# All projections first, one attention pipeline for both sequences, local attention together with the output projection

## The chip, the cores and the metric

The kernel runs on one core of one Trainium2 chip. The metric is the device time of one execution in microseconds (us). The core has a matrix engine, TensorE (PE in the profile; PEld is its loading of weights), and three engines for elementwise work: VectorE (DVE), ScalarE (ACT) and GpSimd (POOL). SyncE (SP) issues the transfers between device memory and the on-chip memory; all of this kernel's transfers stand in its queue. Each engine works off its own instructions in order and waits on semaphores for the others.

## The reference

One encoder layer is applied to two sequences, a prompt of 1024 tokens (s = 0) and a sample of 2048 tokens (s = 1), each with its own condition vector `c`; all data are float32, the model width is 1024. For each sequence:

```python
mod = silu(c) @ w_ada + b_ada
shift, scale, gate = split(mod, 3)
proj = (x * (1 + scale) + shift) @ w_in            # 1024 -> 3328 columns
qa, ka, va, ga, qb, kb, vb, gb = split(proj, ...)  # 512, 128, 128, 512, 4 x 512
oa = window_gqa(qa, ka, va, sink, rel_bias) * silu(ga)
ob = diff_attention(qb, kb, vb, lambdas, subln_w, rel_bias) * silu(gb)
h = concat(oa, ob) @ w_out
y = layer_norm(ALPHA * x + gate * h, ln_g, ln_b)
```

The local attention `window_gqa` has 8 query heads and 2 key heads of 64; a block of 128 queries sees the blocks before, at and after it (384 keys), with a bias by distance, a mask beyond 128 and a sink logit per head that only enters the denominator. The differential attention has 4 heads; each makes two softmaxes over the whole sequence, takes `p0 - lam * p1`, multiplies it with 128 value columns, and normalises the result by its root mean square.

## The kernel before

**Precision.** Each float32 operand of a matmul is split into a high part and a rest (names ending in H and L), and a product is three matmuls: high x high, high x low, low x high. So beside every matmul there is an elementwise split, a copy on ACT and a subtraction on DVE or POOL.

**Stages.** (1) The condition vector becomes shift and scale; tokens are transposed, modulated and split (`build_u`). (2) `projections` runs over three column passes (the prompt, then the two halves of the sample), each over 13 groups of 256 output columns and two blocks of 512 tokens. It is a Python generator whose steps are three matmuls (`step3`, L185 to L187); results go to device memory (`store`). The first pass is run as one piece. (3) `diff_attention(0, ...)` handles the prompt, with three projection steps (`filler(3)`) ahead of each attention step. (4) `window_attention` handles local attention in blocks of 128 queries, in two halves of four heads each: `first` makes logits (L767), adds bias and takes the maximum (L770), takes Exp (L773), and scales by the reciprocal (L791); `second`, one half later, transposes (L810), splits, multiplies with the values (L804, L805), adds the parts of the product (L823, L826), multiplies with the gate (L829) and writes to device memory (OT). Projection steps stand between its parts (`fill(2)`). (5) `diff_attention(1, ...)` handles the sample; it begins among the last projections, and from then on has no filler. One of its blocks (128 queries of one head, L636 to L688) takes four steps on TensorE: logits, values of an earlier pair of blocks, transposes of the block three before. (6) The output projection reads OT, forms the differential half (L929, L930), splits the row block (L936 on ACT, L937 on POOL), multiplies with w_out (L947 to L949), adds the residual and normalises.

**What sets the order.** On TensorE the order is that of the code (`manual_schedule`), so what stands between two attention steps there is written by hand. On the other engines a scheduler orders the instructions at build time. Buffers come from pools of a fixed number of tiles, so a load waits until the last reader of the tile before it is done. The prompt's attention has pools of its own, and local attention and the output projection each open theirs after the pools before them are closed.

Of the kernel before, what the change touches and what calls it, by code (L numbers as in the profile page):

```python
# [66 lines left out]
def hybrid_layer(ctx, tc, x_prompt, x_sample, c_prompt, c_sample, w_in, w_out, w_ada, b_ada, ln_g, ln_b,  # L67
# [28 lines left out]
    for s, S in enumerate(SEQS):  # L96
# [7 lines left out]
        GB.append([dt_([P, S], f"gb{s}_{i}") for i in range(4)])  # L104
        OT.append(dt_([KC, P, S], f"ot{s}"))
# [144 lines left out]
    def store(a, s, t0, kind, i):  # L250
# [8 lines left out]
        elif kind == "vA":  # L259
            vf = ev_p.tile([P, CH], F32, tag="eH", name="vf")  # L260
            nc.vector.tensor_copy(vf, a)
# [289 lines left out]
    def diff_attention(s, lag, filler, early, between, bl, bk, bv, bq, b0, b1, bp, be, bw):  # L551

        S = SEQS[s]
        T = S // P
        NQ = S // CH
        NH = S // 1024
        NJ = 2 * NH
        QG = 256
        NG = HB * T // 2
        LC = min((T - 2) * P, 1024)  # L560
        WL = 2 * LC + 384
        sd = "right" if between else None
        ps_lg = Ring("ps_lg", *bl)
        k_p, q_p, w_p, r1_p, r0_p = Ring("kq", *bk), Ring("q", *bq), Ring("W", *bw), Ring("r1", *b1), Ring("r0", *b0)
        with ExitStack() as st:
            st_p = pool(ctx if between else st, "stat", 8, side=sd)
            for r in (k_p, q_p, w_p, r1_p, r0_p):
                r.open(st, sd)
# [3 lines left out]
            def load_head(h):  # L572
                W = w_p.tile([P, WL], F32, name="W")
                nc.sync.dma_start(out=W[:, LC:LC + 384], in_=toeplitz(HA + h, 1)[:, 0])
                for c0, src in ((0, LC), (LC + 384, LC + 383)):
                    if sum(bw) == 1:
                        nc.scalar.copy(W[:, c0:c0 + LC], W[:, src:src + 1].to_broadcast([P, LC]))
                    else:
                        nc.gpsimd.tensor_scalar(out=W[:, c0:c0 + LC], in0=W[:, src:src + 1].to_broadcast([P, LC]),
                                                scalar1=1.0, scalar2=1.0, op0=ALU.mult, op1=ALU.mult)  # L580
                Kt = []
                for kq in range(NQ):
# [4 lines left out]
                heads[h] = (W, Kt, [])  # L587

            def load_values(h):
                Vt = heads[h][2]  # L590
                for kq in range(NQ):
# [8 lines left out]

            def load_group(gg):
                h, g = divmod(gg, T // 2)
                gs = slice(g * QG, (g + 1) * QG)
# [5 lines left out]
                groups_[gg] = {"Q": Q, "s0": s0g, "PT": []}  # L609

            def logits(t, j):

                gg, b = divmod(t, 2)
                h, g = divmod(gg, T // 2)
                if j == 0 and b == 0:
                    if g == 0:
                        load_head(h)
                    load_group(gg)
                    if t == 0:
                        filler(25 if between else 4)  # L620
                G = groups_[gg]
                W, Kt, _ = heads[h]
                if j == 0:
                    units[t] = {"nm": st_p.tile([P, 2, 2], F32, tag="nm", name="nm"),
                                "s1": st_p.tile([P, 4], F32, tag="s1", name="s1")}
                U = units[t]
                m, hf = 1 - j // NH, j % NH
                if hf == 0:
                    U[m] = (r1_p if m else r0_p).tile([P, S], F32, name=f"l{m}")
                i = g * 2 + b  # L630
# [7 lines left out]
                off = (T - 1 - i) * P + hf * 1024 - (T - 2) * P + LC  # L638
# [21 lines left out]
            def transpose(t, kq):  # L660
                gg, b = divmod(t, 2)
                qs = slice(b * P, (b + 1) * P)
                if b == kq == 0 and gg % (T // 2) == 0:
                    load_values(gg // (T // 2))
                if b == 0:
                    groups_[gg]["PT"].append((pt_p.tile([P, 4, QG], F32R, tag="pth", name="pth"),
# [60 lines left out]
            with tc.manual_schedule(engines={PE}):  # L727
                for n in range(early):
                    slot(n, 5)
                if between:  # L730
                    between()
# [284 lines left out]
```

## Time and profile before

| | |
|---|---|
| median of 3 runs | 2158.64 us (2157.99 to 2159.78) |
| the profiled execution | 2160.91 us; its span, from first to last instruction, 2159.1 us |
| TensorE busy | 2072.7 us (96%), 11597 matmuls |
| DVE, ACT, POOL busy | 1435.0, 1055.3, 1122.8 us (66, 49, 52%) |
| mean granted TensorE clock | 0.989 of 2.4 GHz |
| stages, as TensorE shows them | first pass to 341 us; prompt's attention with projections to 691; local attention with projections to 1243; last projections and first blocks of the sample to 1340; sample's attention to about 1850; output projection to 2159 |

A matmul's record is longer than the time after which the next can start, so that records overlap and the busy time is their union. In the lists a row begins with the line of the kernel; `a<-b,c` names the tile that is written and those that are read. Releasers behind an arrow are what ended an engine's idle time.

### The profile page before, as it was taken

What the parts mean: (1) busy time and instruction counts of PE and PEld (TensorE: products, weight loads), DVE (VectorE), ACT (ScalarE), POOL (GpSimd) and SP (SyncE); (2) the same over time, 40 slices, a digit from 0 to 9 for tenths busy, and PEclk for the clock granted to TensorE, in tenths of its full rate; (3) what the DMA queues carried; (4) which work ended last, traced back from release to release, by engine and by line L of the source; (5) the groups of instructions that cost most, each with busy time, mean ns of one, the idle gap of its engine ahead of it and who ended that gap; (6) DMA issues with size and microseconds to landing.
All of it is one profiled execution on the core that took longest, in us unless ns stands there. A gap on an engine that the chain in (4) does not pass through costs nothing. (4 is left out here: it accounts for less than half of the span.)

```text
span 2159.1 us, 32652 instructions
## 1 busy us (share of the span) xinstructions
PE 2072.7 (96%) x11597; PEld 1778.1 (82%) x11597; DVE 1435.0 (66%) x2753; ACT 1055.3 (49%) x1998; POOL 1122.8 (52%) x780
## 2 busy tenths in 40 slices
PE   7999999998999899999999999999999999899997
PEld 4777898787787798888888987999999999777776
DVE  6334126564562586576566845999999999578887
ACT  6211115454452475455555734777777777422221
POOL 3214125554553232332232334889898888756665
PEclk9999999999999999999999999999999999999999
DMA  9675645554557876585768634123151221756663
GB/s 277 182 279 149 176 132 174 122 115 108 126 116 146 182 210 180 168 202 154 182 165 215 167 112 121 43 85 76 40 115 50 60 67 33 201 175 196 194 177 115
DMA packets 315242, 312.45 MB, mean 145 GB/s; under 512 B 31702, under 2 KB 271990, under 8 KB 314696
## 3 DMA queue, kind: packets, MB, share of 16 engines
q1 hardware_dynamic: 315080, 310.37, 53.2%
q8 instruction: 92, 1.51, 0.4%
q14 instruction: 70, 0.57, 0.1%
HBM read 212.70 MB, written 97.60 MB: 144 GB/s over the span
## 5 line engine op out<-in xcount | busy, mean ns | idle before, releaser
L185 PE MATMUL pj<-uH,wH 128*128 128x512 f32 x1040 | 421.0, 405 | 8.0 <-DVE gg L256 4.8
L187 PE MATMUL pj<-uH,wL 128*128 128x512 f32 x1040 | 410.3, 395 | 0.0
L186 PE MATMUL pj<-uL,wH 128*128 128x512 f32 x1040 | 409.5, 394 | 0.0
L636 PE MATMUL lg<-kt,Q 128*128 128x512 f32 x1280 | 372.5, 412 | 19.5 <-DMA kt<-kb 13.0
L658 POOL TENSOR_TENSOR l<-l,l 128x1024 f32<-128x1024 f32 (+1 forms) x192 | 390.1, 2053 | 0.0
L647 ACT ACTIVATE l<-l,nm 128x2048 f32<-128x2048 f32 (+1 forms) x192 | 330.9, 1723 | 31.3 <-DVE nm L640 31.3
L216 POOL TENSOR_TENSOR wL<-wr,wH 128x1024 fp32r<-128x1024 f32 x74 | 181.7, 2457 | 280.0 <-DVE wH L214 201.3
L656 POOL TENSOR_SCALAR l<-l,s 128x1024 f32<-128x1024 f32 (+1 forms) x192 | 186.3, 983 | 193.5 <-DVE s L651 135.6
L640 DVE CUSTOM_DVE_ANT_0 l<-lg,W 128x1024 f32<-128x1024 f32 x192 | 233.7, 1217 | 64.9 <-PE lg L636 32.9
L674 ACT CAST pth<-tp 128x512 fp32r<-128x512 f32 x320 | 186.1, 582 | 177.8 <-PE tp L672 174.8
L636 PEld LDWEIGHTS lg<-kt,Q 128*128 128x128 f32 x1280 | 222.1, 190 | 58.0 <-DMA kt<-kb 8.7
L185 PEld LDWEIGHTS pj<-uH,wH 128*128 128x128 f32 x1040 | 197.7, 190 | 44.3 <-DVE gg L256 5.7
L187 PEld LDWEIGHTS pj<-uH,wL 128*128 128x128 f32 x1040 | 197.1, 190 | 44.2
L675 DVE TENSOR_TENSOR ptl<-tp,pth 128x512 fp32r<-128x512 f32 x320 | 209.0, 685 | 30.9 <-ACT pth L674 30.9
L186 PEld LDWEIGHTS pj<-uL,wH 128*128 128x128 f32 x1040 | 198.0, 190 | 34.1
L672 PE MATMUL tp<-ident,l 128*128 128x128 f32 x1280 | 193.3, 274 | 3.3 <-DVE ptl L675 3.3
L791 POOL TENSOR_SCALAR l<-l,rcA 128x384 f32<-128x384 f32 (+1 forms) x96 | 59.9, 635 | 243.3 <-DVE rcA L784 173.5
L688 PE MATMUL ac<-pth,vt 128*128 128x256 f32 x640 | 182.2, 285 | 0.2 <-DMA vt<-vb 0.2
L687 PE MATMUL ac<-ptl,vt 128*128 128x256 f32 x640 | 181.6, 284 | 0.6 <-DVE ptl L675 0.6
L686 PE MATMUL ac<-pth,vt 128*128 128x256 f32 x640 | 181.3, 283 | 0.5 <-DMA vt<-vb 0.5
L640 DVE CUSTOM_DVE_ANT_0 l<-lg,W,nm 128x1024 f32<-128x1024 f32 x128 | 164.0, 1282 | 24.9 <-PE lg L636 17.8
L770 DVE CUSTOM_DVE_ANT_0 l<-lgA,tA,nsink 128x384 f32<-128x384 f32 (+1 forms) x192 | 113.7, 593 | 81.6 <-PE lgA L767 77.4
(157 smaller groups left out, 4169.8 us busy)
## 6 DMA issues: line engine op xcount, KB each, us to landing
wr<-in_w_in SPq DMA_DIRECT2D x39, 1024.0 KB, 6.8
KAt<-ka SPq DMA_DIRECT2D x40, 384.0 KB, 6.4
Q<-qb SPq DMA_DIRECT2D x96, 128.0 KB, 3.3
Q<-qb SPq DMA_DIRECT2D x48, 256.0 KB, 3.1
kt<-kb SPq DMA_DIRECT2D x24, 512.0 KB, 4.6
vt<-vb SPq DMA_DIRECT2D x48, 256.0 KB, 5.7
QAt<-qa SPq DMA_DIRECT2D x24, 512.0 KB, 7.4
oraw<-ot SPq DMA_DIRECT2D x12, 1024.0 KB, 6.0
```

Source lines behind the costliest of these rows:

```text
L185: nc.tensor.matmul(acc, lhsT=a(k), rhs=b(k), start=(k == 0), stop=False)
L186: nc.tensor.matmul(acc, lhsT=a(k), rhs=bl(k), start=False, stop=False)
L187: nc.tensor.matmul(acc, lhsT=al(k), rhs=b(k), start=False, stop=(k == KC - 1))
L636: nc.tensor.matmul(L[:, c * CH:(c + 1) * CH], lhsT=G["Q"][:, v, m, qs], rhs=Kt[hf * 2 + c][:, m, :], start=(v == 0), stop=(v == 1))
L640: nc.vector.tensor_tensor_reduce(out=row[:, hf * 1024:(hf + 1) * 1024], in0=L, in1=W[:, off:off + 1024], scale=1.0, scalar=3e38 if hf == 0 ...
L647: nc.scalar.activation(row, row, AF.Exp, bias=nm[:, m, NH - 1:NH], scale=-1.0, accum_out=sums)
L656: nc.gpsimd.tensor_scalar(out=U[1][:, cs], in0=U[1][:, cs], scalar1=s1[:, 2:3], scalar2=1.0, op0=ALU.mult, op1=ALU.mult)
L658: nc.gpsimd.tensor_tensor(out=row[:, cs], in0=row[:, cs], in1=U[1][:, cs], op=ALU.add)
L672: nc.tensor.transpose(pt[:, c * P:(c + 1) * P], units[t][0][:, kb * P:(kb + 1) * P], ident)
L674: nc.scalar.copy(H[:, :, qs], p3)
L675: nc.vector.tensor_tensor(out=L[:, :, qs], in0=p3, in1=H[:, :, qs].bitcast(F32), op=ALU.subtract)
L688: nc.tensor.matmul(a, lhsT=Vt[kq][:, 1, c, :], rhs=H[:, c, :], start=False, stop=(kb == T - 1))
```

## The change

The order of the stages becomes: the first pass, then all of the second and nine groups of the third pass alone; then one differential attention pipeline over the blocks of both sequences, sample first, whose first blocks are mixed with the last four projection groups as before; then local attention and output projection in one loop over 24 blocks of 128 tokens. In that loop block t makes its logits and softmax, block t - 1 its transposes and values, and block t - 2 its output projection. OT's window half no longer goes through device memory: the gate product is split into `oH` and `oL` on the spot. The output projection works on 128 tokens at a time, so its loads are halved and doubled in number. Smaller edits go with it: the factor 0.5 of the window's gate moves into va, the norm's weight `wsub` into rows of w_out, the sink becomes the first element of the row that Exp sums, and the scalings of the softmax go to POOL and ACT alone.

```diff
-    diff_attention(0, 2, fill, 0, None, (1, 0), (2, 0), 2, (2, 0), (3, 0), (2, 0), 3, 1, (1, 0))
...
-            window_attention(wp, tA, 0, range(8))
-            project_until(1, 13)
-            window_attention(wp, tA, 1, range(7))
-            project_until(2, 5)
-            window_attention(wp, tA, 1, range(7, 16))
...
-    diff_attention(1, 3, fill, 3, projected, (1, 1), (4, 2), 5, (2, 0), (3, 1), (3, 0), 7, 2, (1, 1))
+    with tc.manual_schedule(engines={PE}):
+        project_until(1, 13)
+        project_until(2, 9)
+    xst.close()
+    diff_attention((1, 0), 3, 3, projected)
...
+        blocks = [(s, h, i) for s in order for h in range(HB) for i in range(SEQS[s] // P)]
...
             def slot(n, extra):
+                gg, ph = divmod(n - lag - 2, 2)
+                nl, nt = steps_of(n), steps_of(n - lag)
+                nv = steps_of(2 * gg) if 0 <= gg < N // 2 else 0
+                for j in range(max(nl, nt, nv, 2)):
+                    if extra:
+                        fill(extra)
+                    if j < nl:
                         logits(n, j)
+                    if j < nv:
+                        values(gg, ph * nv + j)
+                    if j < nt:
                         transpose(n - lag, j)
...
+        def load_weights(k):
+            for n in range(2):
+                ns = slice(n * 512, (n + 1) * 512)
+                raw = wr_p.tile([P, 512], F32, tag="wr", name="raw")
+                nc.sync.dma_start(out=raw, in_=w_out[k * P:(k + 1) * P, ns])
+                if k >= 4:
+                    nc.vector.tensor_scalar(out=raw, in0=raw, scalar1=wsub, scalar2=None, op0=ALU.mult)
+                nc.scalar.copy(woH[k][:, ns], raw)
+                nc.gpsimd.tensor_tensor(out=woL[k][:, ns], in0=raw, in1=woH[k][:, ns].bitcast(F32), op=ALU.subtract)
...
+                if h4 == 3:
+                    rc = sA_p.tile([P, 4], F32, tag="rc", name="rcA")
+                    nc.vector.reciprocal(out=rc, in_=sm_)
+                    for q in range(4):
+                        lv, r1 = l[:, q, 1:1 + nk], rc[:, q:q + 1]
+                        if q == 1:
+                            nc.scalar.activation(lv, lv, AF.Copy, scale=r1)
+                        else:
+                            nc.gpsimd.tensor_scalar(out=lv, in0=lv, scalar1=r1, scalar2=1.0, op0=ALU.mult, op1=ALU.mult)
+                yield
...
             if n == 1:
                 nc.gpsimd.tensor_tensor(out=og, in0=og, in1=B["G"], op=ALU.mult)
+                split(B, 0, og)
...
+        def split(B, half, o):
+            if "oH" not in B:
+                B["oH"] = o_p.tile([P, KC, P], F32R, tag="oH", name="oH")
+                B["oL"] = o_p.tile([P, KC, P], F32R, tag="oL", name="oL")
+            hs = slice(half * 4, half * 4 + 4)
+            nc.scalar.copy(B["oH"][:, hs, :], o)
+            nc.gpsimd.tensor_tensor(out=B["oL"][:, hs, :], in0=o, in1=B["oH"][:, hs, :].bitcast(F32), op=ALU.subtract)
...
+            nc.gpsimd.tensor_tensor(out=o, in0=o, in1=F, op=ALU.mult)
+            nc.gpsimd.tensor_tensor(out=o, in0=o, in1=gt, op=ALU.mult)
+            split(B, 1, o)
...
+                for k in range(KC):
+                    nc.tensor.matmul(a, lhsT=oH[:, k, :], rhs=woH[k][:, ns], start=(k == 0), stop=False)
+                    nc.tensor.matmul(a, lhsT=oH[:, k, :], rhs=woL[k][:, ns], start=False, stop=False)
+                    nc.tensor.matmul(a, lhsT=oL[:, k, :], rhs=woH[k][:, ns], start=False, stop=(k == KC - 1))
+                    if k < KC - 1:
+                        yield
...
+        outs = outputs()
+        seconds = [iter(()), iter(())]
         with tc.manual_schedule(engines={PE}):
+            for t in range(NB + 2):
+                if t < NB:
+                    Bs[t] = load(*order[t])
...
+                if 1 <= t <= NB:
+                    gather(Bs[t - 1])
+                for n in range(2):
+                    f = first(Bs[t], n) if t < NB else iter(())
+                    for _ in range(4):
+                        next(f, None)
+                        if t > 1:
+                            next(outs, None)
+                        next(seconds[0], None)
+                        if t > 1:
+                            next(outs, None)
+                    for _ in seconds[0]:
+                        pass
+                    seconds = [seconds[1], second(Bs[t], n) if t < NB else iter(())]
```

Where instructions stand on an engine is shown at two places. The lines are those of each kernel; in brackets stands the engine whose semaphore an instruction waits for. First TensorE, where a pair of window values ends (`ac<-ptlA,VAt`; pth and ptl are the two parts of the weights, lgA the logits, po the output). Before, projection steps (pj) follow:

```order
L804 MATMUL ac<-pthA,VAt 128x512 [waits Activation_49]
L805 MATMUL ac<-ptlA,VAt 128x512 [waits DVE_49]
L767 MATMUL lgA<-KAt,QAt 128x384 x2
L185 MATMUL pj<-uH,wH 128x512
L186 MATMUL pj<-uL,wH 128x512
L187 MATMUL pj<-uH,wL 128x512
L185 MATMUL pj<-uH,wH 128x512
L186 MATMUL pj<-uL,wH 128x512
L187 MATMUL pj<-uH,wL 128x512
```

In the changed kernel, where a block's last values end, L848 and L849 are these values, and L912 to L914 the output:

```order
L848 MATMUL ac<-pthA,VAt 128x512 [waits Activation_49]
L849 MATMUL ac<-ptlA,VAt 128x512 [waits DVE_49]
L912 MATMUL po<-woH_15800,oH 128x512
L913 MATMUL po<-woL_15808,oH 128x512
L914 MATMUL po<-woH_15800,oL 128x512
L821 MATMUL lgA<-KAt,QAt 128x384 [waits DMAHW6_49,DMAHW5_49,DMAHW0_49]
L821 MATMUL lgA<-KAt,QAt 128x384
L912 MATMUL po<-woH_15793,oH 128x512 [waits Activation_49]
L913 MATMUL po<-woL_15801,oH 128x512
L914 MATMUL po<-woH_15793,oL 128x512 [waits Pool_49]
```

The first three output matmuls are the last of block t - 2; the three at the end are the first of block t - 1, whose window half comes out of the values above them. Second POOL, around the gate product of a window block (`ogA<-ogA,GAt`). Before:

```order
L791 TENSOR_SCALAR l<-l,rcA 128x384 [waits DVE_49,Activation_49]
L791 TENSOR_SCALAR l<-l,rcA 128x384 [waits Activation_49]
L829 TENSOR_TENSOR ogA<-ogA,GAt 128x512 [waits DMAHW6_49,DVE_49]
L791 TENSOR_SCALAR l<-l,rcA 128x384 [waits DVE_49,PE_49,Activation_49]
L791 TENSOR_SCALAR l<-l,rcA 128x384 [waits PE_49,Activation_49]
```

In the changed kernel L836 are the scalings by the reciprocal, L872 is the gate product, L882 makes a half of oL, L929 is the power of the layer norm:

```order
L836 TENSOR_SCALAR l<-l,rcA 128x384 [waits DVE_49,PE_49]
L836 TENSOR_SCALAR l<-l,rcA 128x384 [waits Activation_49] x2
L882 TENSOR_TENSOR oL<-oraw,oH 128x512 [waits PE_49,Activation_49]
L872 TENSOR_TENSOR ogA<-ogA,GAt 128x512 [waits DMAHW6_49,DVE_49]
L929 TENSOR_TENSOR ve<-ve,mhalf 128x1 [waits DVE_49]
L882 TENSOR_TENSOR oL<-ogA,oH 128x512 [waits Activation_49]
L896 TENSOR_TENSOR oraw<-oraw,F 128x512 [waits DMAHW1_49]
```

Before, the gate product ended a block, and a transfer to device memory followed it; now the split of its result follows, and the differential half's split and three scalings stand ahead of it.

## Rows read from the trace of the kernel before

**Rows 1.** By stage: us, engines' busy us (instructions), granted clock, DMA share, GB/s

```profile
0.00:341.00 341.00, 321.29 (x1612) 259.02 (x1613) 125.62 (x161) 75.76 (x111) 91.23 (x44) 0.99 0.65 197
341.00:1243.00 902.00, 867.18 (x4755) 745.85 (x4753) 555.21 (x1304) 472.40 (x1075) 360.97 (x321) 0.98 0.65 161
1243.00:1840.00 597.00, 592.23 (x3880) 535.53 (x3880) 510.04 (x980) 427.62 (x703) 473.83 (x297) 1.00 0.28 74
1840.00:1906.00 66.00, 55.66 (x315) 46.99 (x314) 36.96 (x48) 25.53 (x45) 42.26 (x23) 0.95 0.67 187
1906.00:2159.10 253.10, 236.38 (x1042) 190.69 (x1040) 207.13 (x263) 53.97 (x65) 154.56 (x98) 0.98 0.57 172
```

**Rows 2.** Timeline of TensorE; start us, length us, line, tiles, count

```profile
1599.92 1.17 PE L636 MATMUL lg<-kt,Q 128*128 128x512 f32 x4
1600.93 0.28 PE L686 MATMUL ac<-pth,vt 128*128 128x256 f32 x1
...
1601.65 0.60 PE L672 MATMUL tp<-ident,l 128*128 128x128 f32 x4
1602.01 1.17 PE L636 MATMUL lg<-kt,Q 128*128 128x512 f32 x4
...
1885.69 0.39 PE L947 MATMUL po<-woH,oH 128*128 128x512 f32 x1
...
1894.99 0.39 PE L949 MATMUL po<-woH,oL 128*128 128x512 f32 x1
```

**Rows 3.** Groups, ACT, 1380 to 1830 us: count, busy us, mean ns, idle

```profile
L647 ACT ACTIVATE l<-l,nm 128x2048 f32<-128x2048 f32 x107 | 214.9, 2008 | 0.0
```

**Rows 4.** Groups of POOL, short sequence's attention, 360 to 690 us

```profile
L658 POOL TENSOR_TENSOR l<-l,l 128x512 f32<-128x512 f32 x64 | 83.7, 1327 | 0.0
L656 POOL TENSOR_SCALAR l<-l,s 128x512 f32<-128x512 f32 x64 | 44.0, 700 | 112.1 <-DVE s L651 106.3 <-PE pj L187 4.0 <-DMA qb<-eH 1.9
```

**Rows 5.** Timeline, the end of one window block: ACT, DVE, POOL

```profile
1002.43 0.58 ACT L823 COPY tmpA<-ac 64x512 f32<-64x512 f32 x1
...
1003.31 0.84 DVE L826 TENSOR_TENSOR ogA<-ac,tmpA 64x256 f32<-64x256 f32 x2
...
1004.24 1.30 POOL L829 TENSOR_TENSOR ogA<-ogA,GAt 128x512 f32<-128x512 f32 x1 [5.87 <-DVE ogA L826]
```

**Rows 6.** Groups of POOL in the window stage, 740 to 1240 us

```profile
L791 POOL TENSOR_SCALAR l<-l,rcA 128x384 f32<-128x384 f32 x78 | 50.4, 657 | 205.3 <-DVE rcA L784 146.4 <-PE pj L187 41.9 <-PE ac L804 9.9
```

**Rows 7.** Timeline, the bias table's load on SP and its first use on DVE

```profile
681.68 0.53 SPq L750 DMA_DIRECT2D tA<-tbl  x1
...
706.36 0.47 DVE L770 CUSTOM_DVE_ANT_0 l<-lgA,tA,nsink 128x256 f32<-128x256 f32 x1
```

**Rows 8.** Timeline, output stage: the split on ACT and POOL

```profile
1937.57 1.05 ACT L936 CAST oH<-oraw 128x1024 fp32r<-128x1024 f32 x1 [7.79 <-POOL oraw L930]
...
1938.70 2.39 POOL L937 TENSOR_TENSOR oL<-oraw,oH 128x1024 fp32r<-128x1024 f32 x1 [1.16 <-ACT oH L936]
```

**Rows 9.** Timeline of TensorE after idle time, which stands in brackets

```profile
472.94 1.19 PE L636 MATMUL lg<-kt,Q 128*128 128x512 f32 x4 [2.97 <-DVE nm L640]
...
1900.30 0.80 PE L947 MATMUL po<-woH,oH 128*128 128x512 f32 x1 [4.93 <-DVE y L950]
...
1905.02 0.39 PE L949 MATMUL po<-woH,oL 128*128 128x512 f32 x1
```

**Rows 10.** View by stretch, as in rows 1, after three idle times

```profile
1900.30:1904.80 4.50, 4.50 (x11) 3.58 (x12) 4.42 (x6) 1.52 (x2) 3.99 (x2) 0.50 0.21 53
509.30:515.50 6.20, 6.15 (x19) 4.85 (x20) 0.53 (x1) 2.04 (x3) 0.00 (x0) 0.50 0.75 245
472.90:479.00 6.10, 6.06 (x35) 5.33 (x36) 4.42 (x10) 3.33 (x7) 4.43 (x5) 1.00 0.37 77
```

**Rows 11.** Timeline of TensorE, its last matmul

```profile
2147.32 0.28 PE L949 MATMUL po<-woH,oL 128*128 128x256 f32 x1
```

More of the change, by code (lines that the diff above doesn't have):

```diff
@@ L103, in hybrid_layer @@
         VB.append([dt_([S, 512], f"vb{s}_{i}") for i in range(2)])
[L104 to L105 removed]
+        GB.append(dt_([4, P, S], f"gb{s}"))
+        OT.append(dt_([HB, P, S], f"ot{s}"))
     brow = dt_([12, NREL], "brow")
@@ L575, in load_head @@
                 for c0, src in ((0, LC), (LC + 384, LC + 383)):
[L576 to L580, printed above, removed]
+                    nc.gpsimd.tensor_scalar(out=W[:, c0:c0 + LC], in0=W[:, src:src + 1].to_broadcast([P, LC]),
+                                            scalar1=1.0, scalar2=1.0, op0=ALU.mult, op1=ALU.mult)
                 Kt = []
-                for kq in range(NQ):
+                for kq in range(SEQS[s] // CH):
                     ks = slice(kq * CH, (kq + 1) * CH)
@@ L586, in load_head, with load_values @@
                     Kt.append(kt)
[L587 to L591, printed above, removed]
+                heads[s, h] = (W, Kt, [])
+            def load_values(s, h):
+                Vt = heads[s, h][2]
+                for kq in range(SEQS[s] // CH):
                     ks = slice(kq * CH, (kq + 1) * CH)
@@ L753, in window_attention, with projected @@
-    def window_attention(wp, tA, s, blocks):
-        S = SEQS[s]
-        T = S // P
-        def first(i, n, B):
-            lo, nk, boff = B["lo"], B["nk"], B["boff"]
-            nm = wp["st"].tile([P, 4], F32, tag="nm", name="nmA")
-            sm_ = wp["st"].tile([P, 4], F32, tag="sm", name="smA")
-            ls = []
+                for n in range(early, N + lag + 4):
+                    slot(n, 0)
+    def projected():
+        project_until(2, 13)
+        pst.close()
+    with tc.manual_schedule(engines={PE}):
+        project_until(1, 13)
+        project_until(2, 9)
@@ L798, in second @@
+                yield
+        def second(B, n):
+            nb, l = B["nb"], B["l"][n]
             O = ac()
@@ L851, in window_attention @@
-        prev = iter(())
-        for i in blocks:
-            B = load(i)
-            if i == 0:
-                fill(12)
-            for n in range(2):
-                for h4, _ in enumerate(first(i, n, B)):
-                    fill(2)
-                    if h4>0:
-                        next(prev, None)
-                        fill(0)
-                for _ in prev:
-                    fill(3)
-                prev = second(i, n, B)
-        fill(5)
-        for _ in prev:
-            fill(2)
@@ new lines, in hybrid_layer, with outputs @@
+        order = [(s, i) for s in (1, 0) for i in range(SEQS[s] // P)]
+        NB = len(order)
+        Bs = {}
+        def outputs():
+            for t in range(NB):
+                yield from output(Bs[t], t == NB - 1)
+                del Bs[t]
+                yield
+        outs = outputs()
+        seconds = [iter(()), iter(())]
+        with tc.manual_schedule(engines={PE}):
+            for t in range(NB + 2):
+                if t < NB:
+                    Bs[t] = load(*order[t])
+                if t == 0:
+                    for k in range(KC):
+                        load_weights(k)
+                    nc.sync.dma_start(out=gbc, in_=ln_g.partition_broadcast(P))
+                    nc.sync.dma_start(out=bbc, in_=ln_b.partition_broadcast(P))
+                if 1 <= t <= NB:
[12 more added lines that the diff above has]
+                    seconds = [seconds[1], second(Bs[t], n) if t < NB else iter(())]
+            for _ in outs:
+                pass
```

398 lines of the change are left out of this document (170 added, 228 removed).

## The prediction

> **What bounds the kernel now.** I read the page's first two parts, then a table by stage, then the waits of TensorE, then single stretches of the timeline. TensorE is the engine that is nearly always busy. Of its 86 us of idle the table by stage shows 20 before 341 us, 35 while the short sequence's attention and then local attention are mixed with projections, 5 in the long sequence's attention (nearly all where it begins), 10 between it and the output projection, 17 in the output projection with the tail [rows 1]. So a new order of stages has little to win: it moves TensorE's work, it doesn't remove any.
>
> What a matmul costs must be read from starts, not from durations, since they overlap. 512 columns start 0.227 us apart (42 matmuls from 1885.69 to 1894.99), 256 columns 0.12 (six from 1600.93 to 1601.65), four transposes take 0.36 [rows 2]; 384 columns I put at 0.17, in proportion.
>
> **Part by part, as times on TensorE.**
> Until 341 us the program is the same: 341.
>
> The projections of the other two thirds now run alone: 2 x 22 x 48 matmuls of 512 columns and 2 x 384 of 256, so 2112 x 0.227 + 768 x 0.12, and 128 transposes x 0.09: 583. The weight splits on DVE and POOL and the weight DMAs hide behind them, as they do in the first third, where DVE is busy 126 of 341 us and POOL 91 [rows 1]. With 7 for the handover into attention (5 idle before): 590.
>
> The long sequence's attention keeps its pipeline. 107 Exp rows in the 450 us from 1380 to 1830, two to a block, make 8.41 us a block [rows 3]; 64 blocks: 538.
>
> The short sequence loses its filler. Alone a block needs two steps on TensorE, 2 x 2.09 (1599.92 to 1602.01) = 4.2 us [rows 2]. POOL needs two scalings of 512 at 0.700 and two sums at 1.327, 4.05, and its share of a power for each second block and two bias fills for each head [rows 4]; with those I take 4.7, and POOL bounds: 32 x 4.7 = 150. Bounds: 4.2 gives 134; 5.5 (POOL and DVE slowing each other) gives 176.
>
> The start of the joint stage has no filler either. POOL must make 16 halves of the low weights, with gathers, splits and scalings in between: 28 instructions of 128x512 at 1.30 and 12 scalings at up to 0.657, 44 us, some 6 of them during the drain [rows 5, 6]. It passes its first scaling only when the bias table tA has landed and a first softmax is done. I take 15 us for that; before, tA was issued at 681.68 and first used at 706.36, 25 us later, with other work between [rows 7]. So TensorE ends its first eight output steps some 53 us after the drain, with 16 us of work in them: 37 idle, 10 more in the drain itself as before [rows 1], 3 for the clock: 50. Bounds: 21, twice the idle of that row, and 62, with tA as late as before.
>
> Then the steady joint stage. Its work on TensorE is 320 x 0.17 + 64 x 0.12 + 544 x 0.09 + 272 x 0.227 for the windows and 1128 x 0.227 + 48 x 0.12 for the output, 434 us, 18.5 a full block. But the new order puts a wait into each block. The values of a window block end with L849. TensorE then has three output matmuls and two logits, and the next one, L912, needs oH, and L914 oL, of that very block. From the start of L849 that is 4 x 0.227 + 2 x 0.17 = 1.25 us of work. What L912 needs comes over a chain of three engines, which the trace has piece by piece [rows 5, 8]: the matmul's own 0.39, copy on ACT 0.58, two sums on DVE 0.84, gate product on POOL 1.30, cast to oH on ACT (1.05 for 1024, so 0.55 here), hand-offs of up to 0.09 each: 3.95 us. For oL comes one more subtraction on POOL: 5.3 us. That bounds the stall from below, 2.7 + 0.9 = 3.6 us.
>
> POOL's order makes it longer. Ahead of the gate product stand three scalings at 0.657 [rows 6], which wait for the reciprocal of the window whose last logits left TensorE 1.25 us before L849, and the other half's subtraction, 1.30. After those logits come 0.53 for the matmuls to end, 0.61 on DVE, some 0.8 for Exp with its sum on ACT and the reciprocal, so the scalings begin about 1.1 us after L849's start. They last until 3.1, the subtraction until 4.4, the gate product until 5.7, the cast until 6.35, and the second subtraction, with a power before it, until 7.7. TensorE stands from 1.25 to 6.4 and again for 0.85: 6.0 us. Queued behind L912 is all the rest, since the order on TensorE is fixed.
>
> After such a gap the clock falls. After 4.93 us of idle the granted clock was 0.50 (1.2 GHz) for 4.5 us of matmuls, which then start 0.43 apart; another stretch at 0.50 lasted 6.2 us; after 2.97 us of idle it stayed at 1.00 (2.4 GHz) [rows 9, 10]. The first cost 2.2 us (11 starts from 1900.30 to 1905.02, 4.7 us instead of 2.5), the second half of its 6.2. I take 2.5 a block.
>
> The Trainium skill's page TensorE: Matmul & The Clock Gate (section HAM oscillation — how this bites in real kernels) describes a loop that stops the array once a round and pays the lower clock in every round. By that rule all 23 rounds here pay, 58 us; by the row of 2.97 us none would.
>
> 23 output blocks begin behind such a wait: 23 x (6.0 + 2.5) = 196, and 0.5 a block, 12, for small waits inside it. The tail after the last matmul keeps its code: 2147.32 to 2159.1, 12 [rows 11].
>
> **Sum.** 341 + 590 + 538 + 150 + 50 + 434 + 196 + 12 + 12 = 2323 us of span. The profiled execution took 2160.91 for its 2159.1, so 2325; it lies 2.3 above the median of 2158.64, which is less than any bound here.
>
> Edits that I cost at nothing: the factor of a half moved into va and w_out (va's copy becomes a scaling; eight scalings of 512 fall into a stretch that POOL bounds), the sink as one more element of Exp (four small DVE and ACT instructions fewer in each half block), GB in one DMA instead of four, OT without its window half. They lie on DVE, ACT and SP, which have room while TensorE or POOL bounds; without that cover, a microsecond or two in each of 24 blocks.
>
> **Rivals.**
> 1. The chain at the block's end is covered. Then the 196 fall away and the removed idle is left: 2127 + 2 = 2129, faster by 1.4%. For it: DVE, ACT and POOL have room in the stage. Against it: the cover is 1.25 us and the shortest chain 3.95. It decides if stall and clock together stay under (2160.9 - 2129) / 23 = 1.4 us a block.
> 2. The stall comes, but the clock stays up, as after 2.97 us: 2325 - 58 = 2267. Against it: the gap that I work out is 5.1 us, longer than the one of 4.93 after which it fell.
> 3. POOL is free when the sums come: stall 3.6, clock 1.7, 23 x 5.3 = 122 instead of 196: 2251. Against it: the order on POOL is fixed too.
> 4. POOL and DVE slow each other where three engines share the block's end: stall 8, clock 3.1, 23 x 11.1 = 255: 2384.
> That the change doesn't do what it says is excluded by the rows of TensorE's order.
>
> **How the numbers follow.** Forecast 0.50, rival 1 0.07, rival 2 0.15, rival 3 0.14, rival 4 0.14. The likeliest is 2325. By its own bounds (short sequence -16 to +26, start -29 to +12) the forecast spans 2280 to 2363; the range takes in rivals 2 to 4 with part of the same bounds, 2235 to 2400, and leaves out rival 1 and the far ends. A measurement here can tell 0.2%, about 4 us, from no change. Faster 0.07; within 0.2% 0.02 (rival 1 with some 1.4 us left in each block); slower 0.91.
>
> **What would show it.** In the profile after: TensorE idle before L912 and L914, with ACT and POOL as releasers, some 23 times 5 and 1 us; a granted clock near 0.9 over the last 650 us; about 27.5 us a block there; the short sequence at 4.7 us a block with POOL near full; 341 us until the first pass ends, as before. I am wrong if L912 hardly waits, or if the lost time lies in the short sequence's attention or the projections.

## The result, and the profile after

The changed kernel takes 2376.64 us (median of 4 runs, 2371.94 to 2380.61), the kernel before 2159.21 beside it: a ratio of 1.1006, with a 95% interval of 1.0985 to 1.1028. Slower was forecast, with 2325 us; the time lies inside the range and 52 us above the forecast. The profiled execution has a span of 2374.4 us.

The page first: what TensorE and POOL are busy, and the dearest waits of TensorE (columns as in part 5: count, busy us, mean ns, idle time ahead and its releaser).

```profile
PE 2144.9 (90%) x11597; PEld 1824.3 (77%) x11597; DVE 1272.8 (54%) x2507; ACT 1047.3 (44%) x2022; POOL 1227.1 (52%) x954
...
L912 PE MATMUL po<-woH,oH 128*128 128x512 f32 (+1 forms) x392 | 176.9, 451 | 101.7 <-ACT oH L881 101.7
...
L914 PE MATMUL po<-woH,oL 128*128 128x512 f32 (+1 forms) x392 | 171.5, 437 | 23.6 <-POOL oL L882 21.6
```

The same 11597 matmuls are busy 72 us longer and idle 143 us longer than before: part of the time is a slower clock, the larger part waiting. The table by stage, with the columns of [rows 1], says where. The cuts are the first pass, the projections with the first blocks of the sample, the sample's attention with the first blocks of the prompt, the rest of the prompt's, the start of the joint stage, the joint stage, the tail.

```profile
0.00:341.00 341.00, 323.14 (x1615) 260.00 (x1616) 125.53 (x162) 74.95 (x110) 93.27 (x46) 0.99 0.63 188
...
341.00:962.00 621.00, 616.42 (x3151) 524.33 (x3150) 180.85 (x253) 113.36 (x175) 167.60 (x82) 1.00 0.48 140
962.00:1492.00 530.00, 529.35 (x3594) 484.83 (x3593) 487.18 (x939) 414.31 (x696) 465.81 (x297) 1.00 0.29 70
1492.00:1648.60 156.60, 138.53 (x867) 124.21 (x865) 115.14 (x255) 111.82 (x267) 121.93 (x132) 0.91 0.53 96
1648.60:1762.00 113.40, 43.20 (x161) 32.83 (x161) 31.16 (x83) 36.90 (x95) 44.49 (x46) 0.64 0.72 163
1762.00:2343.00 581.00, 473.41 (x2107) 380.87 (x2106) 316.87 (x783) 291.38 (x676) 324.45 (x345) 0.88 0.51 132
2343.00:2374.40 31.40, 20.90 (x116) 17.22 (x114) 16.05 (x34) 4.61 (x8) 9.55 (x9) 0.94 0.13 51
```

From 341 to 1492 us TensorE is full and the clock at 1.00. Then come 18 us of idle in the prompt's attention, 70 in the start of the joint stage and 108 in the joint stage, each with a lower mean clock. In the joint stage the same 27.3 us repeat (the first logits of ten blocks stand from 1789.1 to 2062.1). This is one boundary, on TensorE, POOL and ACT (start, length in us; idle time before it and its end in brackets):

```profile
1788.19 0.39 PE L849 MATMUL ac<-ptlA,VAt 128*128 128x512 f32 x1
...
1789.13 0.51 PE L821 MATMUL lgA<-KAt,QAt 128*128 128x384 f32 x2
1794.07 0.80 PE L912 MATMUL po<-woH,oH 128*128 128x512 f32 x1 [4.42 <-ACT oH L881]
1794.66 0.63 PE L913 MATMUL po<-woL,oH 128*128 128x512 f32 x1
1795.43 0.79 PE L914 MATMUL po<-woH,oL 128*128 128x512 f32 x1
```

```profile
1789.20 1.71 POOL L836 TENSOR_SCALAR l<-l,rcA 128x384 f32<-128x384 f32 x3 [8.08 <-PE po L913]
1790.87 1.27 POOL L882 TENSOR_TENSOR oL<-oraw,oH 128x512 fp32r<-128x512 f32 x1
1792.10 1.26 POOL L872 TENSOR_TENSOR ogA<-ogA,GAt 128x512 f32<-128x512 f32 x1
1793.33 0.57 POOL L929 TENSOR_TENSOR ve<-ve,mhalf 128x1 f32<-128x1 f32 x1
1794.09 1.28 POOL L882 TENSOR_TENSOR oL<-ogA,oH 128x512 fp32r<-128x512 f32 x1 [0.20 <-ACT oH L881]
```

```profile
1793.40 0.62 ACT L881 CAST oH<-ogA 128x512 fp32r<-128x512 f32 x1 [1.16 <-POOL ogA L872]
```

The order on POOL is the one that the sum had worked out: scalings, the other half's subtraction, gate product, power, subtraction. The product that [rows 5] has at 1.30 us takes 1.26 here. Counted from L849's start, the scalings begin after 1.0 us, the product after 3.9, the cast after 5.2, L912 after 5.9. L914's wait is all but gone here, where the two matmuls ahead of it run at half the clock; in six other blocks it is 1.1 to 4.7 us. The clock after this wait, in the view of [rows 10]:

```profile
1794.07:1800.50 6.43, 6.30 (x18) 4.71 (x19) 1.39 (x4) 2.81 (x5) 3.57 (x3) 0.51 0.66 167
```

Half speed, 1.2 GHz, for some 6.4 us, in each of the ten blocks. The rule of the Trainium skill that the prediction weighed (page TensorE: Matmul & The Clock Gate, section HAM oscillation — how this bites in real kernels) is borne out: a loop with one stop a round pays the lower clock in every round.

The start of the joint stage: TensorE's two longest waits and the one ahead of the first output, SyncE's issues, and DVE's first use of the bias table.

```profile
1668.35 1.22 PE L821 MATMUL lgA<-KAt,QAt 128*128 128x256 f32 x4 [18.62 <-DMA KAt<-ka]
1691.87 1.22 PE L821 MATMUL lgA<-KAt,QAt 128*128 128x256 f32 x4 [22.29 <-DVE nmA L823]
...
1727.89 0.79 PE L912 MATMUL po<-woH,oH 128*128 128x512 f32 x1 [12.23 <-ACT oH L881]
```

```profile
1644.40 9.93 SPq L805 DMA_DIRECT2D GAt<-ga  x1
1654.38 0.71 SPq L797 DMA_DIRECT2D KAt<-ka  x1
...
1677.78 0.45 SPq L772 DMA_DIRECT2D tA<-tbl  x1
```

```profile
1691.32 0.49 DVE L823 CUSTOM_DVE_ANT_0 l<-lgA,tA,nsink 128x256 f32<-128x256 f32 x1 [40.48 <-DMA tA<-tbl]
```

The last value matmul of the prompt starts at 1648.5. SyncE issues the second block's gate before the first block's keys, and is held 9.93 us by it; the table is issued 29 us after that value matmul and first used 13.5 us later. Before, it was 25 us from issue to use [rows 7], but behind projections.

### The profile page after: what moved, and what is told of

The parts are those of the page before. It is cut to its first block, busy times and chain, and to the rows that moved or that the text cites. A ratio compares the mean times of both kernels' runs of the same rounds, so it can differ in the third digit from the quotient of the medians.

```text
span 2374.4 us, 32457 instructions
## 1 busy us (share of the span) xinstructions
PE 2144.9 (90%) x11597; PEld 1824.3 (77%) x11597; DVE 1272.8 (54%) x2507; ACT 1047.3 (44%) x2022; POOL 1227.1 (52%) x954
## 5 line engine op out<-in xcount | busy, mean ns | idle before, releaser
L185 PE MATMUL pj<-uH,wH 128*128 128x512 f32 x1040 | 409.6, 394 | 4.2 <-DVE gg L256 4.2
L187 PE MATMUL pj<-uH,wL 128*128 128x512 f32 x1040 | 405.1, 390 | 0.0
L186 PE MATMUL pj<-uL,wH 128*128 128x512 f32 x1040 | 404.7, 389 | 0.0
L631 PE MATMUL lg<-kt,Q 128*128 128x512 f32 x1280 | 382.5, 420 | 17.7 <-DMA Q<-qb 14.4
L912 PE MATMUL po<-woH,oH 128*128 128x512 f32 (+1 forms) x392 | 176.9, 451 | 101.7 <-ACT oH L881 101.7
L826 ACT ACTIVATE l<-l,nmA 128x385 f32<-128x385 f32 (+1 forms) x192 | 115.1, 600 | 189.1 <-DVE nmA L823 185.1
L914 PE MATMUL po<-woH,oL 128*128 128x512 f32 (+1 forms) x392 | 171.5, 437 | 23.6 <-POOL oL L882 21.6
L858 DVE TENSOR_TENSOR ptlA<-tp,pthA 128x512 fp32r<-128x512 f32 x136 | 93.6, 688 | 174.3 <-ACT pthA L856 174.2
L684 PE MATMUL ac<-pth,vt 128*128 128x256 f32 x640 | 182.2, 285 | 0.3 <-ACT pth L670 0.3
```

The lines of the kernel that those rows point to most:

```text
L185: nc.tensor.matmul(acc, lhsT=a(k), rhs=b(k), start=(k == 0), stop=False)
L186: nc.tensor.matmul(acc, lhsT=a(k), rhs=bl(k), start=False, stop=False)
L187: nc.tensor.matmul(acc, lhsT=al(k), rhs=b(k), start=False, stop=(k == KC - 1))
L631: nc.tensor.matmul(L[:, c * CH:(c + 1) * CH], lhsT=G["Q"][:, v, m, qs], rhs=Kt[hf * 2 + c][:, m, :], start=(v == 0), stop=(v == 1))
```

## Experiments

Times are medians. A ratio is to the kernel before, which ran beside each group at 2151.7 to 2153.7 us; the changed kernel's is 1.1006. Since the kernel before took 2159.2 us beside the changed kernel, some 6 us of a difference between an experiment and the changed kernel are not the edit's. Stretches and blocks are read from the profiled executions, which lie up to 13 us from their medians (e1 and e8 12 to 13 below, e5 9 above). Blocks are counted from the first logits of one to those of the next, over the sample's full blocks.

### The wait at the block's end

**The output half a block later** (e1).

```diff
-                if 1 <= t <= NB:
-                    gather(Bs[t - 1])
                 for n in range(2):
+                    if n == 1 and 1 <= t <= NB:
+                        gather(Bs[t - 1])
...
-                        if t > 1:
+                        if (t, n) > (2, 0):
                             next(outs, None)
```

> In the joint stage each block's output projection begins half a block later on TensorE than in the changed kernel (and the differential half is gathered half a block later, so that no buffer is added); same work. Theory A (what is lost per block is the wait for the gated window half of the block just finished, and the clock behind it): half a block is 9 us of matmuls, the chain to oL measured 7.2 us after the last window matmul, so the wait goes, the clock stays at 1.00, a full block takes 18.6 to 19.5 us instead of 27.3, and the time is 2376 - 22 x 8.3 = 2195 us (2180 to 2215). Rival B (the three other engines, of which POOL is busy 15.0 us a block, are in each other's order and bound the stage): the wait moves to other lines, a block takes 22 us or more, 2260 us or more.

2267.89 us, 1.0522 (1.0487 to 1.0556). The wait at L912 is gone and 109 us are won, but a block takes 20 to 27 us, 24.3 on average: another wait has come. One boundary, on TensorE, POOL, SyncE and DVE:

```profile
1824.82 0.50 PE L849 MATMUL ac<-ptlA,VAt 128*128 128x512 f32 x1 [2.64 <-DVE ptlA L858]
```

```profile
1822.15 1.26 POOL L896 TENSOR_TENSOR oraw<-oraw,F 128x512 f32<-128x512 f32 x1 [5.84 <-issue]
1823.37 0.55 POOL L929 TENSOR_TENSOR ve<-ve,mhalf 128x1 f32<-128x1 f32 x1
```

```profile
1818.05 0.39 SPq L891 DMA_DIRECT2D oraw<-ot  x1
```

```profile
1823.95 0.21 DVE L948 TENSOR_SCALAR ve<-mv,ve 128x1 f32<-128x1 f32 x1 [4.62 <-POOL ve L929]
1824.08 0.68 DVE L858 TENSOR_TENSOR ptlA<-tp,pthA 128x512 fp32r<-128x512 f32 x1
```

Read backwards: TensorE waits for ptlA, which stands on DVE behind a scaling of the norm; that waits for POOL's power, which stands on POOL behind the first product of the next differential half; and that stands after 5.84 us of idle. The row names no releaser, but SyncE issued that product's load at 1818.05, only 4.1 us earlier, and at ten other blocks the same wait is put down to this load (56 us). So the reading is that it waits for its load; e13 tests it. Neither theory had this: no engine is full, an unhurried instruction stands ahead of an urgent one.

**The differential half's steps first** (e2).

```diff
-                for k in range(KC):
+                for j in range(KC):
+                    k = (j + 4) % KC
```

> Only the order of the eight output steps is changed: the four of the differential half first, then the four of the window half. Theory A: the first steps then need only the differential half, whose oL was ready 3.0 us after the last logits started; the window half is needed four steps (some 3.8 us of matmuls) later and was ready 6.3 us after. So a wait of about 2.0 to 2.5 us stays, the clock falls seldom or for less, a block takes 20.8 to 23 us: 2229 to 2279 us. Rival B (the other engines put the window half first and the differential half last in their queues, so that the same wait stands in front of the other half): a block stays at 27, 2370 us.

2336.3 us, 1.0843 (1.0817 to 1.087); 27.5 us a block on average. Of the 39 us between the profiled executions 31 are won after the prompt's first block begins (220 us to the end instead of 251). The first half is almost in time, but the window half, four steps later, still comes late, 62 us in 18 waits (L915 is the L914 of the changed kernel):

```profile
1908.05 0.79 PE L915 MATMUL po<-woH,oL 128*128 128x512 f32 x1 [5.29 <-POOL oL L882]
```

```profile
1905.52 1.26 POOL L896 TENSOR_TENSOR oraw<-oraw,F 128x512 f32<-128x512 f32 x1 [4.81 <-DMA oraw<-ot]
1906.73 1.26 POOL L882 TENSOR_TENSOR oL<-ogA,oH 128x512 fp32r<-128x512 f32 x1
```

It is the same product waiting for its load, now ahead of the subtraction for oL. Theory A's size was wrong, and B's reason too.

**Extra matmuls in the wait** (e3).

```diff
+                if c0 == 0 and not end:
+                    for _ in range(18):
+                        nc.tensor.matmul(a, lhsT=woH[0][:, :P], rhs=woH[0][:, ns], start=True, stop=True)
```

> 18 extra matmuls of 512 columns (their result is overwritten) stand on TensorE ahead of each block's first output matmul, where it waits 4.42 us in the changed kernel: 4.1 us of work added, nothing else. Theory A (the wait lets the clock fall, and the 6.8 us at 0.50 cost half their length again): the extra work fills the wait, the clock stays at 1.00, a block takes 18.6 + 4.4 + 0.3 = 23.3 us instead of 27.3, and the time falls by 22 x 3.7 = 80 us to about 2295 in spite of 1690 us x 0.0 of useful work less. Rival B (the clock falls for another reason than the wait): a block stays at 27 us, 2376. Rival C (the wait isn't for a chain that runs beside TensorE): the matmuls come on top, 2376 + 23 x 4.1 = 2470.

(The last half sentence on theory A is a slip; its figure is 2295.) 2336.21 us, 1.0853 (1.0828 to 1.0878): 40 us won with 97 us of matmuls added (23 x 18 x 0.234). Ten blocks take 253.8 us, with the clock at 1.00:

```profile
1774.70:2028.50 253.80, 243.56 (x1182) 196.82 (x1181) 150.94 (x370) 138.01 (x321) 152.39 (x160) 1.00 0.58 151
```

So the fall of the clock comes from the wait, and is paid in every block. A block is 25.4 instead of 23.3, since useful work and small waits, taken as 18.6 and 0.3, come to more (below).

**One subtraction from POOL to DVE** (e6).

```diff
+            e = nc.vector if half else nc.gpsimd
-            nc.gpsimd.tensor_tensor(out=B["oL"][:, hs, :], in0=o, ...
+            e.tensor_tensor(out=B["oL"][:, hs, :], in0=o, ...
```

> The changed kernel with one instruction a block on another engine: the subtraction that makes oL of the differential half goes from POOL to DVE (1.27 us less on POOL ahead of the gate product, 0.7 more on DVE). Theory A (POOL's order is part of the chain that TensorE waits for): the gate product comes 1.27 us earlier, TensorE waits 3.1 to 3.2 us a block instead of 4.42; if the clock falls as before a block takes 26.0 us and the time is 2376 - 22 x 1.3 = 2347 us; if the clock stays up after the shorter wait, 22.7 us and 2275 us. Rival B (the sum on DVE, which now has the subtraction ahead of it, sets the time of the gate product): the wait stays at 4.0 us or more, 2365 us or more.

2333.77 us, 1.0839 (1.0821 to 1.0857). The wait is 3.20 to 3.21 us in twelve blocks running, 1.21 less: POOL's order was that much of it. Ten blocks take 259.1 us, 25.9 each (L913 is the L912 of the changed kernel):

```profile
1861.30 0.50 PE L913 MATMUL po<-woH,oH 128*128 128x512 f32 x1 [3.21 <-ACT oH L881]
```

After 3.2 us of idle the clock still falls; by stretch:

```profile
1862.60:1866.00 3.40, 3.34 (x10) 2.87 (x11) 0.50 (x4) 2.11 (x3) 0.61 (x3) 0.50 1.16 294
```

### What is late next

The six kernels of this part go on from e1.

**A fourth tile for xt** (e5): `x2_p = pool(st, "x2", 4)`, and one tile each for F and gt.

> The kernel of e1 (output half a block later) with four tiles instead of three for the residual's rows xt, and one tile instead of two for F and for the gate gt, to make room. In e1 SyncE waited 96 us in 21 times at the load of xt for the store of an earlier output, and the loads of the differential half stood behind it; POOL waited 105 us for those, and DVE and TensorE behind POOL. Rival B (there are too few tiles for xt): with a fourth tile that wait goes, a block of 23.0 us (mean in e1) becomes 19.5, the time 2268 - 20 x 3.5 = 2198 us. Theory A (it is the order in SyncE's queue: the scheduler puts the load of xt right behind the store that frees its tile, however many tiles there are): the wait stays, 2255 to 2280 us.

2269.7 us, 1.0551 (1.0525 to 1.0577): as A had it. SyncE's wait at that load stays, as the same view of e1 and then of e5 shows:

```profile
SPq L900 <- DMA out<-xt: 92.7, 19, 7.2
```

```profile
SPq L900 <- DMA out<-xt: 94.7, 18, 8.0
```

**SyncE's order by hand** (e8): `tc.manual_schedule(engines={PE, SP})`, loads of K and Q a block ahead, then V, G and the differential half's rows, then xt; each store behind the half block in which its output ends.

> The kernel of e1 with SyncE's order in the joint stage written by hand: loads of keys and queries a block ahead, of the values, gates and the differential half's rows one and a half blocks before their use, the load of xt after them, each store behind the loads of its half block. Theory A (what e1 lost was SyncE's queue: POOL waited for late loads and held DVE's and TensorE's operands): POOL waits for loads no more, a block takes 19.4 to 20.5 us instead of 23.0, and the time is 2268 - 20 x 3 = 2208 us (2185 to 2225). Rival B (POOL, DVE and ACT bound the stage together, POOL with 15 us of work in a block): 22 us or more a block, 2245 us or more. Rival C (the DMA engines bound it: 3.2 MB a block at 175 GB/s are 18 us): as B, with the DMA share near full.

2309.49 us, 1.0732 (1.0714 to 1.075), slower than e1. The store stood too early, and SyncE waited there with all later loads behind it:

```profile
SPq L1011 <- POOL xt L961: 268.3, 19, 21.7
```

**The same with e4's edits** (e9; e4 is below).

> The kernel of e8 with the early bias table and four Q tiles of e4 and four instead of three tiles for the raw weights of the output (two instead of three for og, for room). Theory A (with SyncE's order by hand the loads of the joint stage's start come in the order of their use, and the table is there): the start, 97 us from the drain to the steady stage in the changed kernel, takes 60 to 70; the short sequence gives 14 as in e4: 40 us under e8, about 2165. Rival B (the start is bound by what has to be transferred, 18 MB at 176 GB/s, and comes out as long whatever the order): 10 to 15 us under e8, from the short sequence alone, 2195.

2298.22 us, 1.0681 (1.0664 to 1.0698), 11 us under e8: rival B's size. Where the 11 us come from the traces can't say, for the two profiled executions are equally long (spans of 2296.3 and 2295.7 us). From the last value matmul to the fifth block's first logits it takes 126 us (137 in e8), but the attention ends 10 us later: its first Exp row starts 4.5 us later, and at its first blocks TensorE waits 5.0 us for loads of Q. That wait stands in all four kernels with four tiles for Q (e4, e9, e10, e12) and not in e11, which has two for Q.

**The store two half blocks later** (e10): a list holds the stores until then; four tiles for xt.

> The kernel of e9 with each store two half blocks later in SyncE's order, with four tiles for xt (three raw tiles as before, one tile for tmp, for room), and with the second half of the output's weights behind the loads of the third block. In e8 and e9 SyncE waited 14 us a block at the store for the norm that POOL finishes, and all later loads stood behind it; a block took 24.5 us. Theory A (any wait at the head of SyncE's queue turns into a late load, and that into the stall): with the store's wait gone POOL waits for loads no more, a block takes 19.5 to 21 us, the time is 2298 - 22 x 4 = 2210 us (2185 to 2230). Rival B (with the loads in time POOL, DVE and ACT, each with some 12 to 15 us of work in a block and each in a fixed order, hold one another): 22.5 us or more a block, 2250 us or more.

2261.53 us, 1.0508 (1.0487 to 1.053): 37 us under e9 with all its edits together, blocks of 23.8 us, close to rival B's figure. But the loads still weren't in time: POOL waited 82 us in 18 times for F at the first product, which stood ahead of the power here too, and DVE waited 88 us in 21 times for that power. So this run doesn't decide between the two theories. It left one instruction to move.

**One instruction pinned on POOL, on e1** (e13).

```diff
-            nc.gpsimd.tensor_tensor(out=o, in0=o, in1=F, op=ALU.mult)
+            tc.keep_in_program_order(nc.gpsimd.tensor_tensor(out=o, in0=o, in1=F, op=ALU.mult))
```

> The kernel of e1 with one instruction pinned in POOL's order: the first product of the differential half, which waits for its loads, stands behind the norm's power and sums instead of ahead of them; nothing else. Theory A (TensorE's wait for ptlA in e1 comes from that product: the power stands behind it on POOL, a scaling behind the power on DVE, and ptlA behind that): the wait of 46 us in 28 times goes, a block takes 19.4 to 21 us instead of 23.0, the time is 2268 - 20 x 2.5 to 3.5 = 2198 to 2218 us. Rival B (three engines in fixed orders hold one another whatever stands first; a late product makes oL late instead): the wait moves to the matmuls that read oL, 22.5 us or more a block, 2250 us or more.

2204.61 us, 1.0254 (1.0211 to 1.0297): theory A. Ten blocks take 201.0 us:

```profile
1764.70:1965.70 201.00, 197.80 (x1002) 163.94 (x1001) 146.59 (x370) 137.77 (x321) 153.95 (x162) 1.00 0.79 190
```

TensorE is busy 98% at the full clock, and its one wait in these ten blocks is small:

```profile
PE ac L849 <- DVE ptlA L858: 3.0, 10, 0.4
```

POOL does 15.4 us of work a block, about the 15.2 that it did at 27.3 us a block. The engines beside TensorE were never the bound of this stage; their orders were. SyncE's waits (38 us at the load of xt in these ten blocks) cost nothing now.

**The pin on e10** (e12).

> The kernel of e10 with the same pin. Theory A: the loads come early and nothing waits on POOL ahead of the power: 19.4 to 20.5 us a block, 2261 - 16 x 3.7 - 6 x 1.5 = 2193 us (2180 to 2215), a little under the kernel with the pin alone by the short sequence's 14 us. Rival B: as there, 2245 us or more.

2206.95 us, 1.0239 (1.0216 to 1.0262), no less than the pin alone. So what e10 has beside the pin (SyncE's order by hand, later stores, the early table, four tiles for Q) adds nothing, taken together, that can be measured.

### The short sequence and the start of the joint stage

**An early bias table, four tiles for Q** (e4, on the changed kernel).

```diff
+    tA = pool(ctx, "tA", 1, side="right").tile([P, HA, 384], F32, name="tA")
+    nc.sync.dma_start(out=tA, in_=toeplitz(0, HA))
     diff_attention((1, 0), 3, 3, projected)
...
-... Ring("q", 2, 0) ... Ring("r1", 3, 0)
+... Ring("q", 2, 2) ... Ring("r1", 2, 1)
```

> Two edits in two stretches. (a) The bias table tA is loaded before the attention pipeline into room of its own (the ring r1 has two of its three tiles in front for it). (b) The ring of Q tiles has four tiles instead of two. Theory A: (a) takes away the wait of 22 us at the first softmax of the joint stage, but the weights of the output and the second blocks' loads, which end last at 1737 us, then show: 10 to 20 us won of the 97 between the drain and the steady stage; (b) the waits of TensorE for Q in the short sequence (14 us in seven) go, and the clock's falls behind them: 5.4 us a block become 4.6, 20 us won. Together 2340 us (2330 to 2355). Rival B: the transfers themselves bound the start of the stage (engines of the DMA 80% busy from 1640 to 1745) and POOL bounds the short sequence: nothing is won in either stretch, 2370 us or more.

2378.13 us, 1.1049 (1.1031 to 1.1068): rival B. TensorE's waits for Q are gone, and from the short sequence's first Exp to its last it takes 161 us, 174 in the changed kernel; but in e1, e2, e3, e5, e6 and e13, which leave it as it is, that was 161 to 172 (and 157 in e8, which only orders SyncE's loads for the stage behind it), so no gain is shown. A wait of 10 us for the next head's table came in:

```profile
1522.36 2.06 POOL L574 TENSOR_SCALAR W<-W 128x1024 f32<-128x1024 f32 x2 [10.04 <-DMA W<-tbl]
```

The start won nothing: from the last value matmul to the fifth block's first logits 148 us (140.6 in the changed kernel). The wait for the table turned into waits for queries and for the output's weights.

**Fewer bytes at the start** (e11, on the changed kernel).

```diff
-                raw = wr_p.tile([P, 512], F32, tag="wr", name="raw")
-                nc.sync.dma_start(out=raw, in_=w_out[k * P:(k + 1) * P, ns])
+                if k == 0:
+                    raws[n] = wr_p.tile([P, 512], F32, tag="wr", name="raw")
+                    nc.sync.dma_start(out=raws[n], in_=w_out[k * P:(k + 1) * P, ns])
+                raw = raws[n]
```

> The changed kernel with the bias table loaded early, and with the loads of w_out left out but for its first 128 rows (all eight row blocks of weights are made from those, without the factor wsub): 3.7 MB less to transfer at the start of the joint stage. Theory A (the start is bound by what has to be transferred: 18.4 MB at 176 GB/s between 1640 and 1745 us): 5.2 MB with the table fall away, 30 us, and the start takes 60 to 70 us instead of 97: 2376 - 30 = 2346 us. Rival B (it is bound by POOL's and ACT's work for the 16 halves of the weights, 37 us on POOL): at most 5 to 10 us are won, 2368 us.

2337.34 us, 1.0858 (1.0829 to 1.0887). The stretch just named takes 112.9 us, 27.7 less, where 5.2 MB at 176 GB/s are 30 (137 to 143 in e2, e3 and e6, which leave it as it is). By stretch, first the changed kernel, then e11:

```profile
1648.50:1789.10 140.60, 65.84 (x261) 51.11 (x260) 46.33 (x121) 50.67 (x127) 59.64 (x61) 0.68 0.69 158
```

```profile
1637.20:1750.10 112.90, 61.74 (x262) 48.56 (x261) 40.53 (x112) 50.26 (x127) 59.08 (x61) 0.73 0.75 143
```

POOL and ACT do the same work, so rival B is refuted: the loads make the start long, not the arithmetic. That it is their bytes, theory A, fits in size but isn't shown. The edit also takes away waits of SyncE: in that stretch of the changed kernel it waits 22 us before loads of w_out, 11 of them for POOL's subtractions, which free the raw tiles. And e4, which moves the table's 1.6 MB out of the stretch, isn't shorter (148 us). What the loads' order is worth stays open too: with SyncE's order by hand the stretch takes 137 (e8), with the early table beside it 126 (e9) and 121 us (e12), with neither 120.5 (e1) and 125 (e13).

## Why the prediction was right, and by how much it was off

**The mechanism** was right in place and order: TensorE waits at L912 for the cast of oH, as worked out from [rows 5, 6, 8], in all 24 blocks, 12.2 us in the first, 4.4 to 4.5 in eighteen and 1.1 to 3.0 in five, where the sum had 23 alike. A full block takes 27.3 us where the sum had 27.5. Its parts were less right, so the closeness is in part luck. e13 gives a block without the wait as 20.1, so the changed kernel's is 20.1 + 4.4 wait + 2.8, which is what is left for the clock (half of the 6.4 us at 1.2 GHz would be 3.2); the sum had 18.5 + 6.0 + 2.5 + 0.5. The work was too small because matmuls of 512 start 0.234 us apart here, not 0.227 [rows 2], and 0.31 behind four transposes. The wait was too large because each of POOL's pieces was a little shorter than its row and because L914's part was hidden by the slow clock. The errors cancelled.

**Until 341 us, projections, long sequence:** right. The sample's attention makes 96 Exp rows from 991.4 to 1396.6 us, 8.44 a block (8.41 from [rows 3]), and the prompt's first Exp row starts at 1462.6, where the sum begins that part at 1469. **The tail** takes 8.7 us from the start of the last matmul (12 from [rows 11]):

```profile
2365.69 0.28 PE L914 MATMUL po<-woH,oL 128*128 128x256 f32 x1
```

**The short sequence** was mis-sized: the last value matmul is at 1648.5, where the sum had 1629 with its 10 us of drain, 20 later. That term said that POOL bounds at 4.7 us a block. POOL is busy 122 of 157 us, so it doesn't bound; blocks take 5.1 to 5.5. TensorE waited for the loads of Q (14.4 us, seven times), which two tiles allow only late, and the clock fell after these waits. In the six experiments that leave all up to there as it is, that matmul stands at 1632 to 1644, so 5 to 17 of the 20 are this execution's own.

**The start of the joint stage** was the worst term: 40 us after the drain, with 62 as the upper bound for the whole term; the fifth block's first logits stand 75 us later than work and regular waits alone would put them (140.6, less 48 of matmuls and two waits with their clock, 17). The step that failed is "POOL must make 16 halves of the low weights": POOL was counted and the table's load given 15 us, but keys, queries, table and weights all had to be loaded there, 18 MB. e11 shows that the loads set the length, with POOL's work as it was; how much of that is bytes and how much is SyncE waiting for free tiles stays open.

Together 20 + 35 - 3 (tail) = 52, about the span less the sum (2374.4 - 2323 = 51); over the rest of the joint stage the errors cancel.

**Rivals.** That the chain is covered is refuted; e13 is what the kernel would be if it were, and even that is 2.5% slower than before, where the rival had 2129: the rival took over the sum's small terms for the start, the short sequence and the block's work. That the clock stays up is refuted, and so is its ground: [rows 10] shows no fall after 2.97 us, but e6 shows one after 3.21 and the changed kernel after 1.87. That POOL is free when the sums come is refuted by the order, and its effect confirmed by e6. That POOL and DVE slow each other is not seen: DVE's sum lasts 0.42 us in both kernels, POOL's gate product 1.27 (1.29 before).

**Not settled:** why the short sequence takes 161 us in one execution and 174 in another of the same instructions, hence what more tiles for Q are worth; and how the 2.5% that e13 still loses divides over the start and the short sequence.

## What to carry to other kernels

Where stages are joined so that one block's result feeds the next stage at once, count the chain over the slower engines from the last matmul that makes it to the first that reads it, in the order in which each engine will meet its instructions, and put at least that much matmul work between them. When that wait is gone, look for the instruction that waits for a load at the head of a queue with urgent work behind it: pinning one behind the urgent work was worth 63 us here. A stage that opens its buffers after the one before has closed starts with all its loads at once; size it by its loads, not by its arithmetic alone.

## What was not expected of the hardware

The clock fell after idle times shorter than the 2.97 us of [rows 9, 10]. In the prompt's attention of the changed kernel:

```profile
1523.70 1.02 PE L668 MATMUL tp<-ident,l 128*128 128x128 f32 x4 [1.87 <-POOL l L653]
```

```profile
1524.30:1527.60 3.30, 3.30 (x14) 2.91 (x14) 2.69 (x6) 1.83 (x3) 3.30 (x5) 0.55 0.27 23
```

And the slow stretch was not the same each time: after 3.2 us of idle in e6 it lasted 3.4 us in some blocks and 6.8 in others.
